# Two-block transformer kernel on one core: norm sums, transposes and up-projections queued at other places among the projections, and the pairs of one attention swapped

## The chip, the cores and the metric

The kernel runs on one core of a Trainium2 chip. The metric is the device time of one launch in microseconds; three runs and one profiled execution of the kernel before are shown.

## What is computed

One sequence of 512 positions of width 1024, all in 32-bit floats, passes two layers of a first block and then one layer of a second block. The change touches the first block alone. Cut to what matters:

```python
def first_block(x, ...):
    for l in range(2):
        h = rms_norm(x, norm1[l])
        a_cq, a_ckv, a_kr, b_q, b_k, b_v, c_q, c_k, c_v, c_qi, c_ki, c_w, d_q, d_k, d_v, d_f = split_cols(h @ w_in[l])
        # A: latent attention, 4 heads
        qa = rms_norm(a_cq, mla_q_norm[l]) @ mla_w_uq[l]
        kv = rms_norm(a_ckv, mla_kv_norm[l]) @ mla_w_ukv[l]
        o_a = causal_block_attention(cat(qa, rope), cat(kv, rope(a_kr)), kv)
        # B: sliding window of 128, sinks
        o_b = sliding_window_attention(rope(b_q), rope(b_k), b_v, swa_sinks[l])
        # C: an indexer picks the 128 best keys of each query
        o_c = dsa_attention(rope(c_q), rope(c_k), c_v, rope(c_qi), rope(c_ki), c_w, top_k=128)
        # D: causal, with the summed log of a forget gate as bias
        o_d = causal_block_attention(d_q, d_k, d_v, log_f_cum=cumsum(log_sigmoid(d_f + fox_b_f[l])))
        x = x + cat(o_a, o_b, o_c, o_d) @ w_out[l]
        h2 = rms_norm(x, norm2[l])
        x = x + square(relu(h2 @ w_up[l])) @ w_down[l]
    return rms_norm(x, final_norm)
```

Every attention has four heads of 64, worked on as two pairs, 0 and 1. The second block (a gated delta rule, dilated window attention, an output projection) follows and is left as it is.

## The kernel before

Activations lie transposed: 128 features on the partitions, 512 positions in the free dimension, so x is eight tiles `xT`. A 32-bit product is made of three matmuls: a weight is split on the chip into a rounded high part `whi` (ScalarE, L130) and the rest `wlo` (VectorE, L133, or GpSimd, L135, by a table `los`), an activation likewise into `hh` and `hl` (`fold`, L166 and L167). `gemm` (L149 to L153) issues high by high, high by low, low by high for each of the `nk` slices of 128: 24 matmuls of 512 columns for an input projection, 6 or 3 for an up-projection of A. Its target comes from `gtile`, three PSUM buffers for all products. Raw weights pass two buffers, split weights three; `rot`, six buffers, holds evacuated projections.

The norm's gain is folded into the activations; the factor per position is applied when a product is evacuated. For it the squares are summed over the tiles on GpSimd (`sumsq_add`, L178), a matmul with ones sums over the partitions (`rstd_rep`, `ssp`, L185; for one column per position `rstd_nat`, `ssn`, L198), and ScalarE makes the root.

The order of the work is that in which the steps are called, refined by a scheduler that goes by priorities: `cur_priority` of the issue, which `later` lowers for a matmul by `self.gp`, so that matmuls with inputs at hand come between those of a step that waits. Each engine works strictly through its resulting list. The steps `e_...` of `attn` are called by the string of names in its last lines. What the change touches among them:

- `e_rstd` makes the norm factor of the layer's start, used by all evacuations.
- `e_small` evacuates `misc` (index keys, gates, rotary key), sums the gates over the positions (L494) and transposes `misc` (`mt`, L501).
- `e_A2` makes A's latents (`latent`, `lat` and their squares `lt`, L606, L609), their norm factors (`rsq`, `rsk`, `rkn`), and the up-projections (`qn`, `kn`, `qr` and four value blocks, L654 to L656), evacuated at L432.
- `e_D(p)` loads, projects and evacuates D's query and key of pair `p`.
- `values` makes the values of D and C (`DV`, `CV`): four blocks of 128 positions, 24 matmuls of 256 columns each (L568 to L572), evacuated by ScalarE (L574).
- `e_Astack`, `e_Cstack`, `e_Dstack` copy a pair's query and key by DMA into a tile `st` and cast them to high and low parts that lie above one another (`qs`, `kh`, `kl`, L364 to L369), so that two matmuls (L392, L393) make a score block. A's low part `al` is made by GpSimd (L676), its scores are at L686.
- `e_topk` picks C's keys with 16 rounds of VectorE instructions for each block of positions (L549 to L551); the result is C's bias, `score[i]`.
- `e_Aatt(p)` to `e_Datt(p)` do the attention of a pair: for each of four blocks and each of two heads scores, bias and row maximum on VectorE (L315), exponential on ScalarE (L316), transposes (L319), product with the values (L328).
- `e_out` makes the output projection from the tiles `mh`, `ml` of the heads and adds it to x (L810). The first half, B and C left out, runs before C's attention, the second half behind it. Each finished `xT` is squared, summed and folded for the feed-forward part, whose first projection starts on the slices that are there; the sum over the partitions (`ssp<-ssq`) comes ahead of it in the program, and the scheduler puts it where its row stands below.

## Time and profile before

| | us |
|---|---|
| runs | 2155.71, 2148.6, 2143.53 |
| median of the runs | 2148.6 |
| the profiled execution | 2142.94 |
| its span on the core | 2141.2 |
| TensorE busy | 2011.2 (94%) |
| VectorE busy | 1303.4 (61%) |
| ScalarE busy | 970.4 (45%) |
| GpSimd busy | 347.0 (16%) |

The rows further down come from this execution. Times are us from the span's start. A timeline row gives start, duration, engine, line, operation and, in brackets, how long the engine had stood idle before it and what ended that. Matmuls overlap, so that one takes longer by its row than the distance to the next. Layer 0 ends at about 672 us, layer 1 at about 1325; each begins with the attention part (some 310 us) and goes on with the feed-forward part.

### The profile page before, as it was taken

The page shows a single profiled execution, that of the slowest core. Times are in us where ns is not written, and L with a number is a line of the kernel's source. Part 1 is how long each engine was busy: PE and PEld are TensorE (multiplying, and loading weights), DVE is VectorE, ACT ScalarE, POOL GpSimd, SP SyncE. Part 2 cuts the span into 40 slices and gives each one's busy share as a digit, 9 for nine tenths or more (in the row PEclk, how much of TensorE's full clock was granted, in tenths as well). Part 3 has the DMA queues.
Part 4 walks back from the last instruction along what each step waited for, and adds up shares of the span by engine and source line. Part 5 has one row for each costly group of instructions (what it writes and reads, how often), then busy time and mean ns, then how long its engine had stood idle before and what let it go on. Part 6 is the DMA issues. An engine that isn't in the chain of part 4 may idle for free.

```text
span 2141.2 us, 27281 instructions
## 1 busy us (share of the span) xinstructions
PE 2011.2 (94%) x10015; PEld 1588.6 (74%) x10015; DVE 1303.4 (61%) x2372; ACT 970.4 (45%) x1769; POOL 347.0 (16%) x282
## 2 busy tenths in 40 slices
PE   7999989999999899999999999899999999999798
PEld 5776768888887676777777888577677677677586
DVE  6598555445435689655665564794694674853664
ACT  4547454233314456554322223654665664735331
POOL 5236320000004227311000001211011011100000
PEclk9999999999999999999999999999999999999899
DMA  6431443233214332343544343232223222344862
GB/s 189 107 103 57 139 142 118 79 99 118 99 59 123 101 101 75 114 159 99 164 131 138 118 138 112 72 96 79 77 70 93 83 73 65 112 128 143 277 219 89
DMA packets 230647, 243.97 MB, mean 114 GB/s; under 512 B 43771, under 2 KB 186026, under 8 KB 230514
## 3 DMA queue, kind: packets, MB, share of 16 engines
q1 hardware_dynamic: 227826, 240.13, 36.4%
q10 hardware_dynamic: 2688, 2.10, 0.3%
q8 instruction: 79, 1.29, 0.3%
q14 instruction: 54, 0.44, 0.1%
HBM read 203.93 MB, written 31.04 MB: 110 GB/s over the span
## 4 chain that ended last, share of the span: by engine, by line
PE 41%; DVE 11%; DMA 5%; ACT 4%; issue 2%; POOL 1%; SPq 0%; DVEq 0%; ACTq 0%; POOLq 0%
PE g L149 10%; PE g L153 10%; PE g L151 10%; DVE wlo L133 2%; ACT whi L130 1%; DMA raw<-in_w_out_dram 1%; PE oT L328 1%; DVE X L1279 1%; DMA raw<-in_ada_w_dram 1%; DVE ada L967 1%; PE oT L1513 1%; DVE pr L1277 1%; PE nt L1174 1%; PE pt L319 1%; PE g L1709 1%
## 5 line engine op out<-in xcount | busy, mean ns | idle before, releaser
L130 ACT ACTIVATE whi<-raw 128x1024 fp32r<-128x1024 f32 (+3 forms) x302 | 297.2, 1000 | 686.4 <-PE g L151 504.0
L149 PE MATMUL g<-hh,whi 128*128 128x512 f32 (+1 forms) x1368 | 548.3, 401 | 5.9 <-ACT whi L130 3.0
L153 PE MATMUL g<-hh,wlo 128*128 128x512 f32 x1368 | 546.3, 399 | 3.9 <-DVE wlo L133 3.9
L151 PE MATMUL g<-hl,whi 128*128 128x512 f32 x1368 | 548.1, 401 | 0.0
L133 DVE TENSOR_TENSOR wlo<-raw,whi 128x1024 fp32r<-128x1024 f32 (+4 forms) x258 | 300.3, 1178 | 108.9 <-ACT whi L130 100.1
L149 PEld LDWEIGHTS g<-hh,whi 128*128 128x128 f32 (+1 forms) x1368 | 260.1, 190 | 63.0 <-issue 4.9
L153 PEld LDWEIGHTS g<-hh,wlo 128*128 128x128 f32 x1368 | 259.8, 190 | 63.0 <-issue 6.5
L151 PEld LDWEIGHTS g<-hl,whi 128*128 128x128 f32 x1368 | 260.4, 190 | 58.0 <-issue 5.6
L149 PE MATMUL g<-sh,whi 128*128 128x512 f32 x512 | 200.6, 392 | 0.0
L151 PE MATMUL g<-sl,whi 128*128 128x512 f32 x512 | 200.2, 392 | 0.0
L153 PE MATMUL g<-sh,wlo 128*128 128x512 f32 x512 | 199.8, 392 | 0.0
L135 POOL TENSOR_TENSOR wlo<-raw,whi 128x1024 fp32r<-128x1024 f32 x44 | 108.0, 2454 | 417.6 <-ACT whi L130 358.9
L890 DVE TENSOR_TENSOR xT<-xT,g 128x512 f32<-128x512 f32 x128 | 87.7, 686 | 136.7 <-PE g L153 136.3
L178 POOL TENSOR_TENSOR ssq<-sq,ssq 128x512 f32<-128x512 f32 x35 | 51.3, 1466 | 436.8 <-ACT sq L177 436.1
L868 DVE SCALAR_TENSOR_TENSOR r<-g,rstd 128x512 f32<-128x512 f32 x64 | 44.2, 691 | 118.5 <-PE g L153 118.0
L153 PEld LDWEIGHTS g<-sh,wlo 128*128 128x128 f32 x512 | 96.4, 188 | 21.1 <-DVE wlo L133 0.7
L149 PEld LDWEIGHTS g<-sh,whi 128*128 128x128 f32 x512 | 96.5, 189 | 20.9 <-issue 0.9
L151 PEld LDWEIGHTS g<-sl,whi 128*128 128x128 f32 x512 | 96.6, 189 | 20.6 <-issue 0.4
L316 ACT ACTIVATE L<-L,mn 128x256 f32<-128x256 f32 (+3 forms) x128 | 68.4, 536 | 19.3 <-DVE mn L315 18.5
L328 PE MATMUL oT<-ptsb,V 128*64 128x128 f32 x592 | 66.9, 287 | 0.1
L324 ACT ACTIVATE ptsb<-pt 128x256 f32<-128x256 f32 (+3 forms) x128 | 51.0, 412 | 32.5 <-PE pt L319 31.6
L149 PE MATMUL g<-yh,whi 128*128 128x512 f32 x112 | 44.7, 404 | 15.7 <-DVE sg L1674 15.7
(447 smaller groups left out, 3318.2 us busy)
## 6 DMA issues: line engine op xcount, KB each, us to landing
raw<-in_w_in_dram SPq DMA_DIRECT2D x46, 1024.0 KB
raw<-in_w_up_dram SPq DMA_DIRECT2D x32, 1024.0 KB
raw<-in_w_down_dram SPq DMA_DIRECT2D x32, 1024.0 KB
raw<-in_ada_w_dram SPq DMA_DIRECT2D x12, 1024.0 KB
raw<-in_w_in_dram SPq DMA_DIRECT2D x22, 512.0 KB
raw<-in_w_out_dram SPq DMA_DIRECT2D x32, 256.0 KB
fd<-f SPq DMA_DIRECT2D x30, 256.0 KB
xd<-xT SPq DMA_DIRECT2D x24, 256.0 KB
```

The source lines that it names most:

```text
L130: nc.scalar.activation(f(hi), src, AF.Copy)
L133: nc.vector.tensor_tensor(f(lw), src, f(hi), ALU.subtract)
L135: nc.gpsimd.tensor_tensor(f(lw), src, f(hi), ALU.subtract)
L149: nc.tensor.matmul(ps, wh, ah, start=first and k == 0, stop=False)
L151: nc.tensor.matmul(ps, wh, al, start=False, stop=False)
L153: nc.tensor.matmul(ps, wl, ah, start=False, stop=last and k == nk - 1)
L178: nc.gpsimd.tensor_tensor(ssq, sq, ssq, ALU.add)
L316: nc.scalar.activation(L[:, :n], L[:, :n], AF.Exp, bias=m, scale=-1.0, accum_out=sm[:, hh, i:i + 1])
L324: nc.scalar.activation(pts_[:, :n], pt[:, :n], AF.Copy)
L328: nc.tensor.matmul(oT[hh * 64:(hh + 1) * 64, i * P:(i + 1) * P], V(hh, j0 + jj), pts[hh][:, jj * P:(jj + 1) * P], start=jj == 0, stop=jj = ...
L868: nc.vector.scalar_tensor_tensor(r, ps, 0.0, rstd, ALU.max, ALU.mult)
L890: nc.vector.tensor_tensor(x, x, ps, ALU.add)
```

## The change

- `gemm` keeps the list of its matmuls, `proj` a list of those lists; `behind(n, m)` issues what stands in it right behind matmul `m` of the `n`-th projection of the layer (both from 0).
- `e_rstd`'s sums come behind matmul 1 of projection 1, the transposes of `misc` behind matmul 20 of projection 4.
- D's load and projections become steps of their own, `Dp:0` and `Dp:1`. `Dp:0` comes before `A2`, whose norm sums are issued behind matmul 4 and one of whose up-projections behind matmul 16 of projection 6, the first of D. The evacuation stays in `D:0`, behind A2 and its stack.
- `values` raises its priority number by one for each block, so that the blocks don't mix.
- C's pair 1 comes before pair 0; the flag `fast` goes with the pair that is now last, and the second half of the output projection takes the tiles in the order 0, 1, 3, 2.
- In the feed-forward part the first chunk issues two projections before its first evacuation, and the norm sum behind matmul 9 of the second.
- `rot` has eight buffers.

```diff
--- before
+++ after
@@ -144,2 +144,3 @@
         old = self.tc.cur_priority
+        mm = []
         for k in range(nk):
@@ -148,8 +149,9 @@
             self.later(old)
-            nc.tensor.matmul(ps, wh, ah, start=first and k == 0, stop=False)
+            mm.append(nc.tensor.matmul(ps, wh, ah, start=first and k == 0, stop=False))
             self.later(old)
-            nc.tensor.matmul(ps, wh, al, start=False, stop=False)
+            mm.append(nc.tensor.matmul(ps, wh, al, start=False, stop=False))
             self.later(old)
-            nc.tensor.matmul(ps, wl, ah, start=False, stop=last and k == nk - 1)
+            mm.append(nc.tensor.matmul(ps, wl, ah, start=False, stop=last and k == nk - 1))
         self.tc.cur_priority = old
+        self.mm = [m.ins for m in mm]
 
@@ -272,3 +274,3 @@
     def rot(self, name):
-        return self.ap.tile([P, T], F32, name=self.nm(name), tag="rot", bufs=6)
+        return self.ap.tile([P, T], F32, name=self.nm(name), tag="rot", bufs=8)
 
@@ -419,4 +421,12 @@
             self.gemm(ps, wv(hi, lw), acts, KD)
+            mms.append(self.mm)
             return ps
 
+
+
+        mms = []
+
+        def behind(n, m):
+            return self.tc.issue_after(mms[n][m])
+
         def pairsel(raw, r, which, nh):
@@ -463,4 +473,5 @@
         def e_rstd():
-            S["rstd"] = rstd = self.rstd_rep([ssq], D, "rstd")
-            S["rnat"] = self.rstd_nat([ssq], D, "rnat", ap)
+            with behind(1, 1):
+                S["rstd"] = rstd = self.rstd_rep([ssq], D, "rstd")
+                S["rnat"] = self.rstd_nat([ssq], D, "rnat", ap)
             for i, (a, b) in enumerate(((self.cos16, "cosr"), (self.sin16, "sinr"))):
@@ -499,4 +510,5 @@
             pt = self.ps.tile([P, T], F32, name=self.nm("mt"), tag="t", bufs=2)
-            for b in range(NB):
-                nc.tensor.transpose(pt[:, HB(b)], misc[:, HB(b)], self.ident)
+            with behind(4, 20):
+                for b in range(NB):
+                    nc.tensor.transpose(pt[:, HB(b)], misc[:, HB(b)], self.ident)
             ptv = pt.rearrange("p (b c) -> p b c", b=NB)
@@ -563,2 +575,3 @@
                 ps = self.gtile()
+                old += 1
                 for k in range(KD):
@@ -617,5 +630,6 @@
             ckvh, sqk = latent(S["ckv"], [gkv[:, l:l + 1]], P)
-            rsq = self.rstd_rep(sqq, MLA_Q, "rsq", pool=ap, tag="tmp", bufs=self.tb)
-            rsk = self.rstd_rep(sqk, P, "rsk", pool=ap, tag="tmp", bufs=self.tb)
-            rkn = self.rstd_nat(sqk, P, "rkn", ap)
+            with behind(6, 4):
+                rsq = self.rstd_rep(sqq, MLA_Q, "rsq", pool=ap, tag="tmp", bufs=self.tb)
+                rsk = self.rstd_rep(sqk, P, "rsk", pool=ap, tag="tmp", bufs=self.tb)
+                rkn = self.rstd_nat(sqk, P, "rkn", ap)
 
@@ -634,3 +648,4 @@
             ps = self.gtile()
-            self.gemm(ps, lambda k: (uh[:, k, 256:384], ul[:, k, 256:384]), lambda k: cqh[k], 2)
+            with behind(6, 16):
+                self.gemm(ps, lambda k: (uh[:, k, 256:384], ul[:, k, 256:384]), lambda k: cqh[k], 2)
             qr_ = evac(ps, "qr_", rsq)
@@ -694,6 +709,8 @@
 
-        def e_D(p):
+        def e_Dp(p):
             raw = self.raw([w_in[:, o + p * P:o + (p + 1) * P] for o in (O_DQ, O_DK)], KD, 256)
-            ts = [evac(proj([(full, raw[:, :, j * P:(j + 1) * P])]), "dq") for j in range(2)]
-            S["D", p] = ts
+            S["D", p] = [proj([(full, raw[:, :, j * P:(j + 1) * P])]) for j in range(2)]
+
+        def e_D(p):
+            S["D", p] = [evac(t, "dq") for t in S["D", p]]
 
@@ -789,6 +806,6 @@
                    lambda h, i, n: self.causal[:, T - n:] if i == 0 else score[i], 64 ** -0.5,
-                   lambda hh, j: VC[:, j, (2 * p + hh) * 64:(2 * p + hh + 1) * 64], fast=p == 1)
+                   lambda hh, j: VC[:, j, (2 * p + hh) * 64:(2 * p + hh + 1) * 64], fast=p == 0)
 
 
-        def e_out(ts, xload, xstore, cols):
+        def e_out(ts, xload, xstore, cols, turn=(0, 1, 2, 3)):
 
@@ -807,3 +824,3 @@
                 ps = self.gtile()
-                self.gemm(ps, lambda k: (hi[:, k, c], lw[:, k, c]), lambda k: S["mix", ts[k]], 4)
+                self.gemm(ps, lambda k: (hi[:, turn[k], c], lw[:, turn[k], c]), lambda k: S["mix", ts[turn[k]]], 4)
                 x = xload(d)
@@ -822,3 +839,3 @@
         env = dict(locals())
-        for s in 'qi misc rstd Aq Ak qi_rope small score:0 A2 Astack:0 D:0 score:1 Aatt:0 score:3 score:2 DV D:1 topk:2 topk:1 topk:3 Astack:1 Dstack:0 Bq Bk Bv Aatt:1 Dstack:1 Datt:0 Bstack:0 Datt:1 Batt:0 Cq Ck Bstack:1 CV Cstack:1 out1:1 out1:3 Batt:1 out1:2 out1:0 Cstack:0 Catt:0 Catt:1'.split():
+        for s in 'qi misc rstd Aq Ak qi_rope small score:0 Dp:0 A2 Astack:0 D:0 score:1 Aatt:0 score:3 score:2 DV Dp:1 D:1 topk:2 topk:1 topk:3 Astack:1 Dstack:0 Bq Bk Bv Aatt:1 Dstack:1 Datt:0 Bstack:0 Datt:1 Batt:0 Cq Ck Bstack:1 CV Cstack:1 out1:1 out1:3 Batt:1 out1:2 out1:0 Cstack:0 Catt:1 Catt:0'.split():
             n, a = (s.split(":") + [None])[:2]
@@ -848,3 +865,3 @@
                 return self.xT[d]
-            self.e_out((2, 3, 4, 5), ld, lambda d, x: self.sumsq_add(ssq2, x, d), range(4))
+            self.e_out((2, 3, 4, 5), ld, lambda d, x: self.sumsq_add(ssq2, x, d), range(4), (0, 1, 3, 2))
             h2 = []
@@ -852,3 +869,3 @@
                 h2.append(self.fold(self.xT[d], self.vec["norm2"][:, l * KD + d:l * KD + d + 1], d))
-            rstd = self.rstd_rep([ssq2], D, "rstd")
+            rstd = None
             NCH = DFF // 512
@@ -858,4 +875,7 @@
             def up(ch):
-                sq = []
-                for f in range(4):
+                nonlocal rstd
+                pss = []
+
+                def project(f):
+                    nonlocal raw
                     if f % 2 == 0:
@@ -864,4 +884,13 @@
                     hi, lw = self.split([(lambda t: t, raw[:, :, (f % 2) * P:(f % 2 + 1) * P])], [P, KD, P])
-                    ps = self.gtile()
-                    self.gemm(ps, lambda k: (hi[:, k, :], lw[:, k, :]), lambda k: h2[k], KD)
+                    pss.append(self.gtile())
+                    self.gemm(pss[f], lambda k: (hi[:, k, :], lw[:, k, :]), lambda k: h2[k], KD)
+                raw, sq = None, []
+                for f in range(4):
+                    if f == len(pss):
+                        project(f)
+                    if rstd is None:
+                        project(1)
+                        with self.tc.issue_after(self.mm[9]):
+                            rstd = self.rstd_rep([ssq2], D, "rstd")
+                    ps = pss[f]
                     r = fp.tile([P, T], F32, name=self.nm("r"), tag="r", bufs=3)
```

`issue_after` puts what is issued in it into the issue order right behind the given instruction.

How the rows of TensorE's list stand at three places of layer 0. First A2 among D's projections. `g` is a product in PSUM with the number of its tile, `hh` and `hl` are high and low part of the folded input, `lat` of the latent, `whi` and `wlo` of a weight; 128x512 is the output. Before:

```order
L149 MATMUL g_451<-hh_182,whi_447 128x512
L151 MATMUL g_451<-hl_183,whi_447 128x512
L149 MATMUL g_636<-lat_581,whi_620 128x512
L532 MATMUL is_546<-ki_533,qi_543 128x256
L532 MATMUL is_552<-ki_533,qi_543 128x384
L149 MATMUL g_653<-lat_581,whi_620 128x512
L151 MATMUL g_636<-lat_581,whi_620 128x512
L153 MATMUL g_636<-lat_581,wlo_621 128x512
...
L151 MATMUL g_636<-lat_587,whi_620 128x512
L153 MATMUL g_636<-lat_587,wlo_621 128x512
L185 MATMUL ssp_597<-lt_579,ones 128x512
```

Now:

```order
L150 MATMUL g_586<-hh_208,whi_582 128x512
L152 MATMUL g_586<-hl_209,whi_582 128x512
L154 MATMUL g_586<-hh_208,wlo_583 128x512
L150 MATMUL g_615<-hh_119,whi_611 128x512
L150 MATMUL g_697<-lat_642,whi_681 128x512
L152 MATMUL g_697<-lat_642,whi_681 128x512
L154 MATMUL g_697<-lat_642,wlo_682 128x512
L150 MATMUL g_697<-lat_648,whi_681 128x512
L152 MATMUL g_697<-lat_648,whi_681 128x512
L154 MATMUL g_697<-lat_648,wlo_682 128x512
L152 MATMUL g_615<-hl_120,whi_611 128x512
L154 MATMUL g_615<-hh_119,wlo_612 128x512
```

Before, the up-projections (`lat`, two of them in turn) begin inside A's last input projection (`g_451`), ahead of any of D; now they stand among D's two projections (`g_586`, `g_615`), one up-projection at a time, and the square sums ahead of them inside `g_586`.

Second, the start of C's attention: `S` is a score block, `kh`, `kl`, `qs` the stacked key and query; kh_2420 belongs to pair 1, kh_2727 to pair 0. Before, among the output projections (`mh`, `ml`):

```order
L151 MATMUL g_2493<-ml_1657,whi_2472 128x512
L153 MATMUL g_2493<-mh_1656,wlo_2473 128x512
L392 MATMUL S_2738<-kh_2727,qs_2726 128x128
L392 MATMUL S_2748<-kh_2727,qs_2726 128x128
L149 MATMUL g_2493<-mh_1830,whi_2472 128x512
L151 MATMUL g_2493<-ml_1831,whi_2472 128x512
L393 MATMUL S_2738<-kl_2728,qs_2726 128x128
L393 MATMUL S_2748<-kl_2728,qs_2726 128x128
```

Now, in the last value block of C (`whi` by `hh`):

```order
L581 MATMUL g_2384<-whi_2297,hh_119 128x256
L583 MATMUL g_2384<-wlo_2298,hh_119 128x256
L394 MATMUL S_2738<-kh_2420,qs_2419 128x128
L394 MATMUL S_2748<-kh_2420,qs_2419 128x128
L585 MATMUL g_2384<-whi_2297,hl_120 128x256
L581 MATMUL g_2384<-whi_2297,hh_130 128x256
L583 MATMUL g_2384<-wlo_2298,hh_130 128x256
L585 MATMUL g_2384<-whi_2297,hl_131 128x256
L395 MATMUL S_2738<-kl_2421,qs_2419 128x128
L395 MATMUL S_2748<-kl_2421,qs_2419 128x128
```

and later pair 0:

```order
L150 MATMUL g_2452<-mh_1830,whi_2431 128x512
L394 MATMUL S_2870<-kh_2727,qs_2726 128x128
L394 MATMUL S_2880<-kh_2727,qs_2726 128x128
L152 MATMUL g_2452<-ml_1831,whi_2431 128x512
L154 MATMUL g_2452<-mh_1830,wlo_2432 128x512
L395 MATMUL S_2870<-kl_2728,qs_2726 128x128
L395 MATMUL S_2880<-kl_2728,qs_2726 128x128
```

The first scores now read pair 1's key and stand 18 matmuls before the end of the value block; pair 0's stand in the second output projection where before they stood in the fourth.

Third, the second norm sum in the first feed-forward projections. Before:

```order
L153 MATMUL g_3226<-hh_3190,wlo_3223 128x512
L149 MATMUL g_3226<-hh_3194,whi_3222 128x512
L185 MATMUL ssp_3214<-ssq_3011,ones 128x512
L151 MATMUL g_3226<-hl_3195,whi_3222 128x512
L153 MATMUL g_3226<-hh_3194,wlo_3223 128x512
L149 MATMUL g_3226<-hh_3198,whi_3222 128x512
```

Now:

```order
L150 MATMUL g_3220<-hh_3210,whi_3216 128x512
L152 MATMUL g_3220<-hl_3211,whi_3216 128x512
L154 MATMUL g_3220<-hh_3210,wlo_3217 128x512
L150 MATMUL g_3249<-hh_3182,whi_3245 128x512
...
L150 MATMUL g_3249<-hh_3194,whi_3245 128x512
L187 MATMUL ssp_3274<-ssq_3011,ones 128x512
L152 MATMUL g_3249<-hl_3195,whi_3245 128x512
L154 MATMUL g_3249<-hh_3194,wlo_3246 128x512
```

The sum stood behind the tenth matmul of the first projection and stands behind the tenth of the second.

## Rows read from the trace of the kernel before

**Rows 1.** Stretches: us, busy us of PE, PEld, DVE, ACT, POOL, clock, DMA, GB/s
```profile
0.00:325.00 325.00, 289.59 (x1570) 224.94 (x1571) 221.60 (x468) 177.19 (x379) 128.28 (x108) 0.95 0.41 121
325.00:672.00 347.00, 347.00 (x1527) 286.63 (x1526) 168.12 (x196) 111.11 (x144) 14.10 (x10) 1.00 0.32 101
672.00:980.00 308.00, 282.83 (x1533) 219.78 (x1532) 208.95 (x454) 164.99 (x362) 110.67 (x85) 0.95 0.36 106
```

**Rows 2.** Waits of PE, whole span: total us, times, longest
```profile
PE ssp L185 <- POOL ssq L178: 11.6, 4, 4.7
PE S L392 <- ACT kh L367: 5.5, 2, 2.8
PE g L149 <- DVE qn L432: 5.5, 2, 2.8
...
PE g L149 <- ACT lat L606: 3.1, 2, 1.5
...
PE S L686 <- POOL al L676: 3.0, 2, 1.5
...
PE S L686 <- DVE mn L315: 2.2, 2, 1.2
PE mt L501 <- issue: 2.1, 1, 2.1
PE mt L501 <- DVE misc L494: 2.0, 1, 2.0
...
PE ssp L185 <- ACT lt L609: 1.9, 2, 0.9
PE S L393 <- POOL kl L369: 1.7, 2, 0.9
```

**Rows 3.** Short stretches behind waits, columns as in rows 1
```profile
134.00:138.00 4.00, 3.94 (x13) 3.65 (x14) 3.79 (x15) 1.48 (x6) 0.00 (x0) 0.50 0.02 4
...
321.00:324.00 3.00, 2.93 (x5) 1.70 (x6) 0.57 (x1) 0.79 (x2) 0.02 (x1) 0.50 0.00 0
...
677.00:681.00 4.00, 4.00 (x14) 3.26 (x15) 0.00 (x0) 1.37 (x4) 2.50 (x2) 0.57 0.00 0
...
728.00:732.00 4.00, 4.00 (x17) 3.61 (x17) 0.93 (x2) 2.08 (x5) 0.00 (x0) 0.50 1.03 231
```

**Rows 4.** Timeline of PE at the start of layer 1: start, us, instruction, idle before
```profile
675.65 0.70 PE L185 MATMUL ssp<-ssq,ones 128*128 128x512 f32 x1 [1.87 <-POOL ssq L178]
```

**Rows 5.** Timeline of DVE and POOL at A2, layer 0
```profile
67.67 2.35 POOL L135 TENSOR_TENSOR wlo<-raw,whi 128x1024 fp32r<-128x1024 f32 x1 [12.29 <-DVE rb L292]
67.69 2.87 DVE L293 TENSOR_TENSOR rb<-qr__135_643,sin 64x512 f32<-64x512 f32 x1
...
72.03 0.69 DVE L432 TENSOR_TENSOR qn<-g,rsq 128x512 f32<-128x512 f32 x1
```

**Rows 6.** Timeline at the second norm sum, layer 0
```profile
319.39 0.70 ACT L166 ACTIVATE hh<-xT,veccol 128x512 fp32r<-128x512 f32 x1
...
320.13 1.44 DVE L167 SCALAR_TENSOR_TENSOR hl<-xT,veccol,hh 128x512 fp32r<-128x512 f32 x1 [0.23 <-ACT hh L166]
...
321.07 2.07 PE L185 MATMUL ssp<-ssq,ones 128*128 128x512 f32 x2 [4.67 <-POOL ssq L178]
...
327.56 0.39 PE L149 MATMUL g<-hh,whi 128*128 128x512 f32 x1
```

**Rows 7.** Timeline at the start of attention C, layer 0
```profile
241.29 1.03 POOL L369 CAST kl<-kl 64x1024 fp32r<-64x1024 f32 x1
...
242.21 0.50 PE L149 MATMUL g<-mh,whi 128*128 128x512 f32 x1 [0.19 <-ACT V L574]
...
254.87 0.69 PE L392 MATMUL S<-kh,qs 128*128 128x128 f32 x2 [2.77 <-ACT kh L367]
```

**Rows 8.** Stretches with top-k rounds, layer 0, columns as in rows 1
```profile
120.00:160.00 40.00, 37.01 (x158) 29.33 (x157) 38.06 (x92) 13.05 (x23) 12.55 (x7) 0.91 0.35 103
...
200.00:236.00 36.00, 35.15 (x229) 26.62 (x230) 31.43 (x92) 18.91 (x55) 11.81 (x7) 1.00 0.19 56
```

More of the change, by code (lines that the diff above doesn't have):

```diff
@@ L692, in e_Aatt @@
                    lambda hh, j: VA[:, j, (2 * p + hh) * 64:(2 * p + hh + 1) * 64])
+        def e_Dp(p):
+            raw = self.raw([w_in[:, o + p * P:o + (p + 1) * P] for o in (O_DQ, O_DK)], KD, 256)
+            S["D", p] = [proj([(full, raw[:, :, j * P:(j + 1) * P])]) for j in range(2)]
         def e_D(p):
-            raw = self.raw([w_in[:, o + p * P:o + (p + 1) * P] for o in (O_DQ, O_DK)], KD, 256)
-            ts = [evac(proj([(full, raw[:, :, j * P:(j + 1) * P])]), "dq") for j in range(2)]
-            S["D", p] = ts
+            S["D", p] = [evac(t, "dq") for t in S["D", p]]
         def e_Dstack(p):
```

## The prediction

> **What bounds the kernel now.** I read four views of the profile, in this order. The table of stretches [rows 1] shows TensorE (PE) at work nearly all the time: in the first feed-forward part, 325 to 672 us, it is busy throughout, 1527 matmuls in 347.00 us, so 0.227 us for each 512-column matmul at full clock and about 0.12 for one of 256. The attention parts of the two layers are the ones with room: 325.00 - 289.59 = 35.4 us without a matmul in the first, 308.00 - 282.83 = 25.2 in the second, and a mean granted clock of 0.95 in both. So PE sets the end, and what the change can win is PE's idle time in the first block and the clock lost behind it. The second block is not touched.
>
> The view of waits names the idle time [rows 2]. Each line has its counterpart in both layers: PE waits for the last square sum (11.6 in four waits), for the casts of a stacked key (5.5 and 1.7), for an evacuated up-projection (5.5), for the normed latent and its squares (3.1 and 1.9), for `misc` (2.0 and 2.1), for the low part of A's stack (3.0). Together 36.4 us. [...] Finally the timelines around four places [rows 4 to 7].
>
> **The change part by part.** The sum is made against the profiled execution, 2142.94 us; the median of the three runs is 2148.6, 5.7 above it.
>
> *Norm sums of a layer's start.* They move 17 matmuls back, about 3.9 us of PE work. In layer 1 PE waited 1.87 us for the sum [rows 4]; 3.9 covers that. The matmuls behind ran at 0.57 for 4.00 us [rows 3], 1.7 lost. Later users of the norm wait for a projection anyway. Layer 0 had only 0.3 (11.6 - 4.7 - 4.7 - 1.9). All of it would be 0.3 + 1.87 + 1.7 = 3.9, without the clock 2.2; I take **3.4**, as PE then has no stop there at all, less a little for what the sums themselves take.
>
> *Transposes of `misc`.* They move behind 12 more matmuls, 2.7 us, against waits of 2.0 and 2.1 [rows 2]: **4.1**, with little doubt, as only the small per-row weights hang on them; if those came late, scores would wait, so the lower end is 2.
>
> *A2 and D.* Before, A's up-projections stand inside its last input projection, ahead of D's two, and PE waits 2.8 + 1.5 + 0.9 = 5.2 us a layer [rows 2]; in layer 1 the clock is then 0.50 for 4.00 us of work [rows 3], 2.0 lost; layer 0 I put at 1.5. After, 48 projection matmuls stand ahead and between, so the inputs are ready. But both `D` tiles now stay in PSUM until A2 has been evacuated, so all up-projections pass one buffer of three: matmuls, evacuation, next. An evacuation takes 0.69 [rows 5]; with the tail of the last matmul I count 1.1. Four projection matmuls between cover 0.9, eleven 2.5, none nothing: three waits of 0.2, one of 1.1, and about 1 for the value blocks behind ScalarE, 2.7 in all. I keep 0.7 of the clock loss. So 5.2 + 1.5 - 3.4 = 3.3 and 5.2 + 2.0 - 3.4 = 3.8, **7.1**. Upper end: no new wait, 13.9. Lower end: a DVE instruction beside POOL's 2.35 us cast took 2.87 instead of 0.69 [rows 5]; two of them more on that chain in each layer take 8.8 off and leave -1.7.
>
> The raw weights of `D` are asked for earlier on SP's queue, those of A2 and the last three copies of the index stack later; the index scores are then some 1.2 us later, but stand deeper among projections, which cover them. At nothing.
>
> *V blocks whole, and A's second pair.* The four V blocks of `DV` now run one after another; fewer fillers stand among the first pair's scores. The second pair's scores start 29 rows, some 6.6 us of PE work, later, which covers the 1.5 us wait for POOL's low part [rows 2]; behind it 2.0 us are lost to the clock [rows 3]. Upper end 2 x 3.5 = 7; lower end 0, as a wait for row maxima (2.2 in two [rows 2]) can grow while DVE is busy 38.06 of 40 us [rows 8]. I take 2 a layer, **4**.
>
> *C's pairs swapped.* Before, PE waits 2.77 us for the high part of pair 0's key and 0.85 (half of 1.7) for the low one [rows 2, 7]. After, pair 1 comes first, and its scores are put into the last V block. Its key's second half is ready at 241.29 + 1.03 = 242.3; PE, which starts the output projection at 242.21 [rows 7], would be 18 matmuls of 0.12 ahead of that, at 239.9: a new wait of 2.4. Pair 0 comes later by one pair's first scores, but sooner than its own key: I count 0.9 and 1.7. That is 5.0 against 3.6, offset by copies that no longer stand behind two stores on SP's queue. **0**, between -6 and +11 for both layers: all of the new against the old, or all gone and 2.0 of clock each.
>
> *Second norm sum.* Before, PE stops behind the tenth matmul of the first feed-forward projection for 4.67 us, until the sum arrives, and runs its next 2.93 us at 0.50 [rows 3, 6]. Now it goes on, until it needs the last folded row: its high part ends at 319.39 + 0.70 = 320.1, its low part at 320.13 + 1.44 = 321.6 [rows 6]. So two waits of some 1.3 us stay, the second projection starts at about 322.3 instead of 327.56, and the sum itself still takes 1.0 there (2.07 at half clock). Gain 5.3 - 1.0 = 4.3; with half clock in 3 us of it 2.8. I take 3.5, twice: **7**.
>
> *Eight rotary buffers* and the changed turn of the sums remove waits only; nothing.
>
> *What is lost on the way.* Up to C, DVE is busy 31.43 of 36 us [rows 8], and the casts of C's keys hang on it. PE arrives there some 8 us earlier in layer 0, and what DVE can't follow comes back as a wait. I take 2 a layer, **-4**.
>
> Sum: 3.4 + 4.1 + 7.1 + 4 + 0 + 7 - 4 = 21.6, so 2142.9 - 21.6 = **2121 us**.
>
> [...]
>
> **The rivals.**
> 1. *All named waits go.* The 36.4 us of [rows 2] and nine half-clock stretches in the attention parts, four of them in [rows 3], at some 1.5 each: 2142.9 - 50 = 2093. For it: the moves are made at just these places. Against: the last folded row and the keys of C are late by themselves [rows 6, 7].
> 2. *The leads are given back at C.* PE waits until DVE and POOL have C's keys; then only the second sum, `misc` in part and layer 1's start remain: 7 + 2 + 3 = 12, 2131. For it: DVE at 0.87 before C. Against: DVE's own waits before C are for PE, so it can move up too.
> 3. *A2 stays at half clock* through the short stops: 2.4 more lost in each layer, 2126. [...]
> 4. *Slower.* The first pair of A has eight score blocks whose maxima DVE makes between top-k rounds, and DV's blocks no longer stand between them. If each block then waits 1.5 us, with a half-clock stretch of 2.0 for every second one, a layer loses 20; two lose 40 and beat the 25.6 won elsewhere: 2143 + 14 = 2157. It decides from about 1 us a block on. Against: the second `D` pair's projections and the index scores fill the place.
> 5. *The change doesn't do what it says:* the order on PE moved as described, so only in that the waits move along: 2143.
>
> **How the numbers follow.** Forecast, 2110 to 2130 (the terms of A2 and C half way to their ends, the others together 1.5 either way): 0.45; rival 1: 0.10; rival 2: 0.20; rival 3: 0.10; rival 4: 0.05; rival 5: 0.10. A measurement of this kernel can tell about 0.5% from no change, so faster means below 2137.9 by the median. The forecast and rivals 1, 2 and 3 lie there, but for a third of rival 2's spread: 0.45 + 0.10 + 0.13 + 0.10 = 0.78. Same: 0.07 + 0.10 = 0.17; slower 0.05. The range leaves out rival 4, half of rival 1 and some of rival 5, whose single time is its upper edge: 2095 to 2143.
>
> **What would show it.** In the changed kernel PE's waits for `misc` and for the first norm sum should be gone; the waits for up-projections be several below 1.2 us; at the second norm sum PE should wait about 1.3 for a high and 1.3 for a low folded part, and the granted clock there be above 0.7; at C a wait for POOL's key of pair 1 should appear. The prediction is wrong if layer 0's attention, up to the first feed-forward part, does not end 8 to 15 us sooner, if waits for row maxima grow by more than 5 us, or if the A2 stretches show a granted clock near 0.5 for more than 3 us.

## The result and the profile after

The changed kernel takes 2121.91 us, the median of four runs from 2117.55 to 2123.68, against 2148.3 before; the ratio is 0.9872, with a 95% interval of 0.9852 to 0.9892. That is 1.3% faster. In a later set of rounds it took 2121.83 us, at 0.9887 (0.9858 to 0.9916). The profiled execution has a span of 2121.4 us, 19.8 below that of before.

PE's waits in the changed kernel (whole span; us in total, times, longest):

```profile
PE g L150 <- DVE sg L1703: 16.5, 1, 16.5
PE S L395 <- POOL kl L371: 6.7, 5, 1.6
PE S L701 <- DVE mn L317: 5.4, 2, 2.7
...
PE S L395 <- POOL qk L385: 3.1, 2, 1.9
...
PE g L669 <- DVE kn L442: 1.8, 2, 0.9
...
PE S L701 <- POOL al L691: 1.5, 2, 0.7
...
PE S L394 <- ACT kh L369: 1.3, 2, 0.7
...
PE g L150 <- DVE qn L442: 0.4, 2, 0.2
```

The waits for the square sum (11.6 before), for `misc` (4.1) and for the latent and its squares (5.0) are gone; those for an up-projection fell from 5.5 to 0.4 and, at the value blocks, 1.8, those for the high part of a key from 5.5 to 1.3 [rows 2]. POOL's low key part is now waited for 6.7 us, where it was 1.7: 6.1 of it at C, 0.6 at one place of B. The wait for row maxima at A has grown from 2.2 to 5.4. The first row lies in the second block and stands in both kernels (15.7 before).

The stretches (us; busy us of PE, PEld, DVE, ACT, POOL; granted clock; DMA; GB/s), first whole attention parts, then short ones:

```profile
0.00:316.00 316.00, 290.18 (x1579) 224.88 (x1580) 221.33 (x468) 176.63 (x378) 127.99 (x108) 0.97 0.42 125
...
660.00:956.00 296.00, 280.09 (x1549) 216.91 (x1548) 206.28 (x456) 165.30 (x362) 111.93 (x86) 0.98 0.37 113
```

```profile
60.00:80.00 20.00, 19.08 (x78) 13.25 (x76) 11.17 (x21) 9.22 (x19) 1.56 (x1) 1.00 0.54 143
80.00:90.00 10.00, 9.34 (x72) 8.85 (x73) 5.39 (x5) 4.87 (x9) 5.98 (x3) 1.00 0.21 53
...
136.00:140.00 4.00, 4.00 (x13) 3.42 (x12) 2.76 (x10) 0.99 (x4) 0.00 (x0) 0.50 0.20 69
312.00:316.00 4.00, 1.95 (x5) 1.35 (x6) 2.26 (x2) 1.64 (x3) 1.40 (x1) 0.81 0.01 4
316.00:320.00 4.00, 4.00 (x13) 2.91 (x12) 1.22 (x1) 0.44 (x1) 0.00 (x0) 0.77 0.26 48
664.00:668.00 4.00, 4.00 (x19) 3.02 (x19) 0.45 (x1) 1.41 (x3) 1.85 (x2) 1.00 0.12 45
```

Without a matmul are 316.00 - 290.18 = 25.8 us of layer 0's attention part, where it was 35.4, and 296.00 - 280.09 = 15.9 of layer 1's, where it was 25.2 [rows 1]. The clock is 0.97 and 0.98 after 0.95. In A2 (60 to 90 us) and at the start of layer 1 (664 to 668) it is 1.00 now; behind A's row maxima (136 to 140) it is 0.50 still, as in [rows 3].

Where the time came from shows best at marks that both traces have. Each mark is the start of one instruction in PE's timeline, the folded rows' in DVE's; "lead" is by how much it comes sooner. A modulation sum is a small matmul for the second block, placed in layer 1's feed-forward part.

| mark | before | changed | lead | won since the mark above |
|---|---|---|---|---|
| layer 0: first matmul of D's values | 87.44 | 82.19 | 5.2 | 5.2 |
| first matmul of C's values | 230.34 | 224.12 | 6.2 | 1.0 |
| last folded row | 320.13 | 313.06 | 7.1 | 0.9 |
| last feed-forward product | 670.66 | 660.65 | 10.0 | 2.9 |
| layer 1: first matmul of D's values | 742.52 | 722.13 | 20.4 | 10.4 |
| first matmul of C's values | 885.16 | 865.24 | 19.9 | -0.5 |
| last folded row | 974.80 | 953.84 | 21.0 | 1.0 |
| first modulation sum | 1007.27 | 983.12 | 24.1 | 3.2 |
| last modulation sum | 1271.05 | 1247.13 | 23.9 | -0.2 |
| last output product | 2133.21 | 2113.46 | 19.8 | -4.2 |

So the starts of the two layers give 15.6 of the 24 us won in the first block, the second norm sums 6, and all of the attention between them 2.4. Four us are lost in the part that was not changed; by the medians of the runs, 2148.3 - 2121.9 = 26.4 us were won, so they are this pair of executions' own.

The second norm sum in the changed kernel, layer 0, by the timeline (start, us, engine, instruction, idle before):

```profile
312.31 0.71 ACT L168 ACTIVATE hh<-xT,veccol 128x512 fp32r<-128x512 f32 x1
...
313.06 1.44 DVE L169 SCALAR_TENSOR_TENSOR hl<-xT,veccol,hh 128x512 fp32r<-128x512 f32 x1 [0.24 <-ACT hh L168]
...
313.07 0.49 PE L150 MATMUL g<-hh,whi 128*128 128x512 f32 x1 [1.20 <-ACT hh L168]
...
314.55 0.80 PE L152 MATMUL g<-hl,whi 128*128 128x512 f32 x1 [0.98 <-DVE hl L169]
...
315.57 0.63 PE L150 MATMUL g<-hh,whi 128*128 128x512 f32 x1
...
318.95 1.02 PE L187 MATMUL ssp<-ssq,ones 128*128 128x512 f32 x2
```

PE does not stop for the sum, which now stands at 318.95, but for the last folded row, 1.20 us for its high and 0.98 for its low part. The second projection begins at 315.57, 2.5 us behind the start of the low part, where it was 7.4 [rows 6].

A2 and the start of C in PE's timeline, and POOL's at C:

```profile
74.07 0.47 PE L150 MATMUL g<-lat,whi 128*128 128x512 f32 x1 [0.19 <-DVE qn L442]
...
80.15 0.36 PE L669 MATMUL g<-whi,lat 128*128 128x256 f32 x1 [0.88 <-DVE kn L442]
```

```profile
233.85 0.41 PE L394 MATMUL S<-kh,qs 128*128 128x128 f32 x2 [0.69 <-ACT kh L369]
...
236.27 0.69 PE L395 MATMUL S<-kl,qs 128*128 128x128 f32 x2 [1.49 <-POOL kl L371]
```

```profile
235.18 1.03 POOL L371 CAST kl<-kl 64x1024 fp32r<-64x1024 f32 x1
```

The up-projections that pass one PSUM buffer cost stops of 0.19 and 0.88 us. At C the low part of pair 1's key ends at 235.18 + 1.03 = 236.2, and PE's second set of score matmuls starts behind it, after 1.49 us of standing idle. With 0.69 for the high part and 1.56 for pair 0's low part, PE waits 3.7 us for C's keys in layer 0; before it was 2.77 + 0.85 = 3.6.

### The profile page after: what moved, and what is told of

It is laid out like the page before. It is cut to its first block, busy times and chain, and to the rows that moved or that the text cites. A ratio compares the mean times of both kernels' runs of the same rounds, so it can differ in the third digit from the quotient of the medians.

```text
span 2121.4 us, 27312 instructions
## 1 busy us (share of the span) xinstructions
PE 2008.2 (95%) x10015; PEld 1584.1 (75%) x10015; DVE 1299.5 (61%) x2372; ACT 970.4 (46%) x1769; POOL 346.6 (16%) x282
## 4 chain that ended last, share of the span: by engine, by line
PE 68%; DVE 14%; DMA 7%; ACT 5%; issue 3%; POOL 1%; SPq 1%; DVEq 0%; ACTq 0%; POOLq 0%
PE g L150 17%; PE g L152 17%; PE g L154 17%; DVE wlo L133 3%; PE oT L330 2%; PE pt L321 1%; ACT whi L130 1%; DVE X L1308 1%; DMA raw<-in_w_out_dram 1%; DMA raw<-in_ada_w_dram 1%; DVE ada L996 1%; PE oT L1542 1%; DMA st<-c 1%; DVE m L561 1%; DVE sc L562 1%
## 5 line engine op out<-in xcount | busy, mean ns | idle before, releaser
L133 DVE TENSOR_TENSOR wlo<-raw,whi 128x1024 fp32r<-128x1024 f32 (+3 forms) x258 | 306.3, 1203 | 114.6 <-ACT whi L130 106.1
L154 PEld LDWEIGHTS g<-hh,wlo 128*128 128x128 f32 x1368 | 259.7, 190 | 62.5 <-issue 6.9
```

What stands on the lines that cost most here:

```text
L133: nc.vector.tensor_tensor(f(lw), src, f(hi), ALU.subtract)
L154: mm.append(nc.tensor.matmul(ps, wl, ah, start=False, stop=last and k == nk - 1))
```

## The experiments

Parts of the change were undone one at a time, one part was put into the kernel before alone, and three versions try what the new waits point at. Times of different rounds are compared by their ratio to the kernel before in the same rounds. A single ratio is sure to some 0.2%, 4 us; the marks of the profiles tell smaller effects apart, where stages in the same order repeat: from the last feed-forward product of layer 0 to the first matmul of D's values in layer 1 the changed kernel needs 61.48 us, and eight other profiles with the same order there 61.46 to 61.99. Other stages repeat less well. From D's values to C's values all kernels but the last one below take 140.3 to 144.9 us, and from C's values to the last folded row all that make C's low key part on POOL take 88.0 to 92.6; smaller differences are not told apart there by one profile.

**A2 back ahead of D.**

```diff
-... score:0 Dp:0 A2 Astack:0 D:0 ...
+... score:0 A2 Astack:0 Dp:0 D:0 ...
-            with behind(6, 4):
-            with behind(6, 16):
```

> The changed kernel with A2 put back ahead of D's projections (its norm sums and up-projections no longer placed among them); all else stays. Theory (the terms add): the waits for the up-projections (2.8 us a layer), for the latent (1.5) and its squares (0.9) come back with a half-clock stretch behind them, so the first value block of D starts about 3.5 us later in layer 0 and the time is 6 to 9 us above the changed kernel's 2122. Rival (slack: what is won early is waited for again at C's keys, where the changed kernel waits 3.0 us a layer for POOL): the C waits shrink by as much, and the time rises by 0 to 3 us only.

2138.17 us, ratio 0.9945 (0.9932 to 0.9959): 0.0073 above the changed kernel's first ratio, some 16 us. The stage named above takes 66.98 us, 5.5 more, and in layer 0 the part from the transposes of `misc` to D's values 39.03 instead of 32.80. PE's waits in layer 1's attention part:

```profile
PE S L395 <- POOL qk L385: 4.4, 1, 4.4
...
PE g L150 <- DVE qn L442: 2.8, 1, 2.8
PE g L150 <- ACT lat L619: 1.5, 1, 1.5
PE S L699 <- POOL al L689: 1.5, 1, 1.5
PE S L699 <- DVE mn L317: 1.4, 1, 1.4
...
PE ssp L187 <- ACT lt L622: 0.9, 1, 0.9
```

The three waits of before are back, 2.8, 1.5 and 0.9. The rival falls: nothing is given back at C, where PE waits 4.2 us for keys in layer 0, not less than the 3.7 of the changed kernel. The theory is short by half: beside A2's own stages (6.2 and 5.5) the copy in D's stack on POOL is waited for 4.0 and 4.4 us in the two layers, where the changed kernel waits 3.1 in both together. The kernel before waited only 1.3 and 0.6 there, so undoing this part alone overstates what it is worth. And the waits at A's second pair are 1.5 for the low part and 1.4 for row maxima, nearly as before (1.5 and 1.2 in this layer), not 0.7 and 2.7: what happens at that pair comes from the A2 part.

**A2's part alone, put into the kernel before** (with eight rotary buffers).

```diff
-... score:0 A2 Astack:0 D:0 ... DV D:1 ...
+... score:0 Dp:0 A2 Astack:0 D:0 ... DV Dp:1 D:1 ...
+            with behind(6, 4):
+            with behind(6, 16):
-        return self.ap.tile([P, T], F32, name=self.nm(name), tag="rot", bufs=6)
+        return self.ap.tile([P, T], F32, name=self.nm(name), tag="rot", bufs=8)
```

> The kernel before with the A2 part alone (D's projections ahead, norm sums and one up-projection placed among them, eight rotary buffers). Theory (its worth is large by itself): the waits of 5.2 us a layer go, layer 1's start up to D's first value block falls from 71.9 to 65 to 67 us, and the time is 9 to 14 us below the kernel before. Rival (the parts need each other: without the later transposes PE stops there, and without the later scores what is won is waited for at C): 4 to 7 us below.

2138.87 us against 2149.13, ratio 0.9958 (0.9942 to 0.9974): 10 us of gain (9 by the ratio, whose interval is 6 to 12 and so doesn't shut out the rival's 4 to 7), and 66.62 us in layer 1's stage, as the theory has it. PE's waits in layer 1's attention part and at the norm sum behind it:

```profile
PE ssp L187 <- POOL ssq L180: 6.8, 2, 4.9
...
PE S L696 <- DVE mn L317: 2.7, 1, 2.7
PE mt L509 <- issue: 2.1, 1, 2.1
...
PE S L696 <- POOL al L686: 0.7, 1, 0.7
```

Here the value blocks are interleaved as before and C's pairs stand as before; the waits at A's second pair are those of the changed kernel, 2.7 and 0.7. That the value blocks cover them, as the prediction said, is not so. In layer 0, from the transposes to D's values, it is 36.67 us where the kernel before needs 39.51: 2.8 won, although this execution lost 1.7 us to a half clock behind the wait for `misc` (0.57 from 52 to 56 us), where the kernel before ran at 1.00. So this part is worth 2.8 and 5.2 us when added alone, 6.2 and 5.5 when undone. Which of its moves does it, D's projections ahead or the sums and the up-projection among them, was not tried.

**The transposes of `misc` back.**

```diff
-            with behind(4, 20):
+            if True:
```

> The changed kernel with the transposes of misc back at their old place. Theory (terms add): the wait of 2.0 and 2.1 us comes back, +4 us, no half-clock stretch. Rival (slack later): projections behind it shield A2 from its own waits, so a stop here makes the latents come in time and the time rises by under 2 us.

2119.43 us, ratio 0.9863 (0.9840 to 0.9885): by the time no difference can be told. By the stage of layer 1, 62.90 us, it is worth 1.4 there.

```profile
PE mt L513 <- issue: 2.1, 1, 2.1
```

The wait of 2.1 is back; one of 0.7 for the index scores' query, which the changed kernel has in this place, goes. So the theory's size is a third too large in that layer. In layer 0, from the first product with `wlo` (at 18.50 us in the changed kernel) to D's values, it is 65.23 us, after 63.69 in the changed kernel and 62.5 to 63.5 in the nine other profiles that have the transposes and A2 where it has them: at least 1.5 more. Together that is some 3 us, nearer to the theory's 4 than to the rival's less than 2.

**The first norm sums back.**

```diff
-            with behind(1, 1):
+            if True:
```

> The changed kernel with the norm sums of a layer's start back at their old place. Theory: in layer 1 a wait of 1.9 us and a half-clock stretch of some 1.5 us return, in layer 0 0.3 us: +3 to +4 us. Rival: PE has more projections ready and the norm is needed by DVE only later, so under +1.5 us.

2126.36 us, ratio 0.9878 (0.9856 to 0.9901). The time again tells little; the stage of layer 1 takes 67.07 us, 5.6 more, which is against the rival. The wait and the stretches behind it (columns as above):

```profile
PE ssp L187 <- POOL ssq L180: 1.9, 1, 1.9
```

```profile
668.00:672.00 4.00, 4.00 (x14) 3.19 (x13) 0.00 (x0) 1.56 (x4) 0.58 (x1) 0.50 0.01 4
672.00:676.00 4.00, 4.00 (x13) 3.15 (x13) 0.65 (x1) 0.93 (x1) 1.94 (x2) 0.69 0.00 0
```

1.9 us of wait and 4.00 x 0.50 + 4.00 x 0.31 = 3.2 of clock make 5.1 of the 5.6. In the kernel before the same wait was followed by 1.7 of lost clock [rows 3], and so it was in the kernel with A2's part alone (0.57 from 677 to 681 us): the wait repeats, the length of the half-clock stretch does not.

**The second norm sum back ahead of the projections.**

```diff
-            rstd = None
+            rstd = self.rstd_rep([ssq2], D, "rstd")
...
-                    if rstd is None:
-                        project(1)
-                        with self.tc.issue_after(self.mm[9]):
-                            rstd = self.rstd_rep([ssq2], D, "rstd")
```

> The changed kernel with the second norm sum issued ahead of the feed-forward projections again. Theory: the wait of 4.7 us for the last square sum and its half-clock stretch come back in both layers, +6 to +7 us together (net 2.9 and 3.2 a layer by the traces). Rival (the folded rows bind anyway): the waits of 1.2 and 1.0 us for the last folded row are what counts, and the time rises by less than 3 us.

2129.49 us, ratio 0.9901 (0.9885 to 0.9918), 0.0029 above the first ratio of the changed kernel, some 6 us, though the two intervals overlap. PE waits for the sum as it did, in layer 0

```profile
PE ssp L187 <- POOL ssq L180: 5.3, 1, 5.3
```

and in layer 1 4.6. From the last folded row to the last feed-forward product it is 349.94 us against 347.59, 2.4 more in layer 0, and 32.18 against 29.28 up to the first modulation sum, 2.9 more in layer 1. The marks separate the two orders: the three profiles with the sum ahead take 349.9 to 350.6 and 32.2 to 32.7 us, the eleven with it behind 346.1 to 348.9 and 27.7 to 29.3. The theory holds by them; the rival does not.

**The value blocks interleaved again.**

```diff
-                old += 1
```

> The changed kernel with the four value blocks interleaved again (priority not raised per block). Theory: it moves the second pair of A earlier, so that the wait for POOL's low part of A (0.7 now, 1.5 before) comes back and the time rises by 1 to 4 us. Rival (whole blocks cost fillers): the wait for row maxima at A's scores, 2.7 us a layer in the changed kernel against 1.0 before, goes away and the time falls by 2 to 5 us.

2126.62 us, ratio 0.9876 (0.9857 to 0.9896): the same. PE's waits at A in layer 1:

```profile
PE S L700 <- DVE mn L317: 2.7, 1, 2.7
...
PE S L700 <- POOL al L690: 0.7, 1, 0.7
```

Both are those of the changed kernel, and layer 0 has the same 2.7, so neither theory nor rival has it right: this line moves neither wait, and the time by nothing that can be measured.

**C's pairs back.**

```diff
-... Cstack:0 Catt:1 Catt:0
+... Cstack:0 Catt:0 Catt:1
-... fast=p == 0)
+... fast=p == 1)
-... range(4), (0, 1, 3, 2))
+... range(4))
```

> The changed kernel with C's pair 0 first again, with the flag and the order of the sums as before. Theory (the swap only trades waits): PE waits for pair 0's key again, 3.6 us or a little more a layer, in place of 3.0 for pair 1's; the time is within 0 to +4 us of the changed kernel. Rival (the swap is what lets the lead through): PE reaches pair 0's scores 6 us earlier than before while its key does not come earlier, so the wait grows to 8 us or more a layer and the time rises by 10 us or more.

2120.49 us, ratio 0.9864 (0.9849 to 0.9879): the same. PE's waits at C, layer 0:

```profile
PE S L394 <- ACT kh L369: 3.4, 1, 3.4
...
PE S L395 <- POOL kl L371: 1.8, 2, 1.2
```

0.6 of the 1.8 lies at B. At C it is 3.4 and 1.2 us in place of 0.7 for the high and 3.0 for the low part of a key. The swap trades one wait for the other, as the theory has it.

**Six rotary buffers.**

```diff
-        return self.ap.tile([P, T], F32, name=self.nm(name), tag="rot", bufs=8)
+        return self.ap.tile([P, T], F32, name=self.nm(name), tag="rot", bufs=6)
```

> The changed kernel with six rotary buffers. Theory (as forecast: they cost nothing and win little): within 2 us of the changed kernel. Rival (they are what lets D's tiles be evacuated while A2's are still in use): evacuations of D wait for a buffer, PE waits at the products behind them, and the time rises by 4 us or more.

2114.81 us, ratio 0.9841 (0.9817 to 0.9865). Not slower, and the stage of layer 1 takes 61.62 us, so the rival falls. By the ratio it is 7 us faster, which is more than the theory's 2; whether six are better is not settled, as the interval overlaps that of the changed kernel.

**The changed kernel again.**

> The changed kernel once more, on the chip and in the rounds of the three beside it, with a second profile. Theory (what differs between executions is the clock behind waits, not the order): its stages from the first matmul of the second block on differ from the first profile by some us (866 us there from the last modulation sum to the last output product), while layer 1's start up to D's first value block is again 61.5 us, within 0.3; the time is 2117 to 2127. Rival: the stages repeat within 0.3 us everywhere, so that stage differences of 3 us between the kernels are real.

2121.83 us. Layer 1's start takes 61.53 us, after 61.48. From the last modulation sum to the last output product it is 870.5 us (1242.14 to 2112.60), after 866.3; before 862.2, and in the other kernels, all with the same code there, 861.6 to 871.5. So the theory holds: the 4.2 us lost in the second block are no effect of the order. The whole stretch in the kernel before, in the changed kernel and in its repetition (columns as above):

```profile
1271.05:2133.21 862.16, 805.00 (x4137) 625.25 (x4137) 527.42 (x989) 430.09 (x773) 93.93 (x79) 0.98 0.37 113
```

```profile
1247.13:2113.46 866.33, 807.43 (x4138) 626.99 (x4137) 528.09 (x989) 429.79 (x773) 93.85 (x79) 0.97 0.37 112
```

```profile
1242.14:2112.60 870.46, 812.18 (x4138) 630.09 (x4137) 528.16 (x989) 430.09 (x773) 93.97 (x79) 0.97 0.36 112
```

PE stands idle 57.2, 58.9 and 58.3 us, and is busy 805.0, 807.4 and 812.2 for the same matmuls, at a mean clock of 0.98, 0.97 and 0.97. So 2.4 of the 4.2 us are slower matmuls and 1.7 longer waits; between the two executions of the changed kernel the matmuls take 4.8 us more and the waits 0.6 less.

**C's low key part on DVE.**

```diff
+        if kv:
+            for r in (slice(0, 64), slice(64, 128)):
+                nc.vector.tensor_tensor(kl[r, :nk], st[64:128, :nk], kh[64:128, :nk], ALU.subtract)
+            return q, kh, kl
         (eng or nc.gpsimd).tensor_tensor(kl[0:64, :nk], st[64:128, :nk], kh[64:128, :nk], ALU.subtract)
         nc.gpsimd.tensor_copy(kl[64:128, :nk], kl[0:64, :nk])
...
-            S["C", p] = self.stack(st, eng=eng("C"))
+            S["C", p] = self.stack(st, eng=eng("C"), kv=True)
```

> The changed kernel with the low key part of C's stacks made on DVE, both halves by subtraction, in place of a 2.4 us subtraction and a 1.0 us copy on POOL; the values are the same. Theory (at C PE waits for POOL's work alone, 3.0 us a layer): these waits shrink to under 1 us each layer and the time falls by 3 to 6 us. Rival (DVE or the high part is as late): a wait for the high part or for row maxima takes their place, and the time stays within 2 us.

2115.07 us, ratio 0.9824 (0.9803 to 0.9846). At C no wait for `kl` is left (B's stacks stay on POOL, with one wait of 0.6); what leads PE's waits in layer 1 now is

```profile
PE S L705 <- DVE mn L317: 2.7, 1, 2.7
PE S L399 <- POOL qk L389: 2.3, 1, 2.3
```

From C's values to the last folded row it takes 85.55 and 85.40 us in the two layers, after 88.94 and 88.60: 6.6 us together, just above the theory's 3 to 6. Both stages lie below the 88.0 to 92.6 of the kernels with POOL's keys. By the ratio it is 10 us.

**The same with C's pair 0 first** (the edits of "C's pairs back" and of the run above).

> The changed kernel with the low key part of C's stacks made on DVE and C's pair 0 first again. Theory (the swap only trades waits): within 3 us of the version with the swap and DVE keys (2115 in its own rounds). Rival (the swap pays once POOL is out of the way, since pair 0's high part is late by its copies): a wait of 3 us a layer for the high part stays, and the time is 5 to 8 us above that version.

2116.88 us, ratio 0.9853 (0.9826 to 0.9881). By the medians that is 2 us above the version with the swap, as the theory has it, by the ratios 6 us, as the rival has it; the intervals overlap, so the time doesn't decide. A wait for the high part of the key stays in layer 1:

```profile
PE S L398 <- ACT kh L369: 2.4, 1, 2.4
```

With 2.0 in layer 0 it is nearer to the rival's 3 us than to nothing; by the stages, 85.95 and 87.25 us, it costs 0.4 and 1.9. So the swap may be worth some 2 us once POOL is out of the way, which is not sure, and before that it can't be told from nothing.

**C's keys on DVE, with the swap, and D's stack copied on ScalarE.**

```diff
-        nc.gpsimd.tensor_copy(kl[64:128], kl[0:64])
+        nc.scalar.activation(kl[64:128], kl[0:64], AF.Copy)
```

> The changed kernel with the low key part of C's stacks on DVE, and the copy within D's stacks on ScalarE in place of POOL. Theory: the waits for D's low key part on POOL (1.0 and 2.3 us in the version with C's keys on DVE) go, and the time falls by 1 to 4 us more, to 2110 to 2116. Rival (ScalarE's list holds the copy back behind exponentials): a wait for ScalarE takes their place and nothing is won.

2104.05 us, ratio 0.9797 (0.9773 to 0.9820), against 0.9887 (0.9858 to 0.9916) for the changed kernel in the same rounds: 18 us faster than it, and 45 than the kernel before. That is more than the theory's 2110 to 2116. PE's first waits in layer 1:

```profile
PE S L705 <- DVE mn L317: 2.7, 1, 2.7
PE is L548 <- POOL qi L542: 1.8, 3, 1.1
```

No wait for POOL's copy is left. From D's values to C's values it takes 139.13 and 138.58 us, after 141.75 and 144.91 in the version with C's keys on DVE alone: 2.6 and 6.3 us, where the waits themselves were 1.0 and 2.3. In layer 1 that version ran at 0.86 in the 25 us around this place, this one at 1.00, so in this pair of executions a half-clock stretch went with the wait. Both times lie below all others of this stage, 140.3 to 144.9, but by 1.2 and 1.7 us only: how much of the gain repeats was not tried.

ScalarE does not make this copy faster than POOL, 1.06 us against 1.03. In layer 1, with C's keys on DVE alone, POOL

```profile
798.73 0.88 POOL L737 TENSOR_SCALAR db<-crep,cumn 128x128 f32<-128x128 f32 x1 [5.57 <-DMA crep<-cumd]
...
800.54 1.03 POOL L389 CAST qk<-qk 64x1024 fp32r<-64x1024 f32 x1
```

and with D's copy on ScalarE

```profile
792.04 1.06 ACT L389 ACTIVATE qk<-qk 64x1024 fp32r<-64x1024 f32 x1
```

But DVE's part of the key was there at 797.84 and POOL began 2.7 us later, as the copy stood behind D's bias (`db`), which had waited for a transfer; in the other version DVE's part was there at 791.45 and ScalarE began 0.6 us later.

## Why the prediction was right

The forecast was 2121, the time is 2122. The sum was 21.6 against one execution; the spans differ by 19.8, the medians by 26.4, the first block by 24. The main mechanism is right: stops of PE at the starts of the layers and at the second norm sum went, and with them most of the half clock behind them: the granted clock is 1.00 at the start of layer 1 and in that layer's A2, where it was 0.57 and 0.50, and 0.81 and 0.77 at the second norm sum of layer 0, where it was 0.50. That the number is within 1 us is in part luck, as the execution it starts from was a quick one: from the median of before, 2148.6, the same sum gives 2127. Its steps did not all come out so well.

- *Starts of the layers* (3.4 + 4.1 + 7.1 = 14.6): 15.6 by the marks. Within it the sizes were off. A2 is worth 2.8 and 5.2 when added alone, 6.2 and 5.5 when undone, for 3.3 and 3.8: the prediction charged 2.7 us a layer for the one PSUM buffer and kept 0.7 of the clock loss; the stops were 0.19 and 0.88 in layer 0, and the clock 1.00. The first norm sums are worth 5.6 in layer 1 when undone, not 3.1, since the half-clock stretch behind the wait was longer there (3.2 us lost, for 1.7). The transposes are worth 1.4 in layer 1 and some 1.5 in layer 0, not 2.05. Undone singly these make 12.5 in layer 1, while together they win 10.4 there, so they are not independent; the sum came out because the errors had both signs. By the times, A2 undone and the second norm sum undone make 16 + 6 = 22 of the 26 us; no other part undone singly can be told from nothing by its time.
- *V blocks and A's second pair* (4): this step failed. The line on the value blocks does nothing that can be measured. That pair's wait for POOL does shrink, from 1.5 to 0.7, but the wait for row maxima grows from 1.0 and 1.2 to 2.7, and both follow from A2, as A2 alone and A2 undone show. Won up to C: 1.0 and -0.5 in this pair of executions, in which a loss for DVE is already contained; the stage varies by more than that.
- *C's pairs* (0) and *what is lost on the way* (-4): the wait for pair 1's key stands where it was foreseen, 0.69 + 1.49 = 2.2 us in layer 0 for 2.4, and pair 0's key is waited for 1.56, for 2.6. Together 3.7 for 3.6 before, so 0 is right. (The lower end of -6 does not come out of the prediction's own numbers: 5.0 against 3.6 is -2.8 in two layers.) Won from C on 0.9 and 1.0, less than this stage varies, and nothing was taken back: undoing A2 made C no quicker. The -4 has no counterpart of its own; with the 4 above it cancels, which is luck.
- *Second norm sum* (7): 2.9 and 3.2 by the marks, 2.4 and 2.9 when undone; the waits of 1.3 and 1.3 are 1.20 and 0.98, and the clock 0.81 and 0.77 there, as said.
- *Rotary buffers* (0): the eight win nothing that can be seen; six were not slower, and whether they are quicker is open.
- *Second block* (0): -4.2 in this pair of executions, 2.4 of it by the clock and 1.7 by waits; the repeated profile shows that it is no effect of the change.

Of the signs named ahead, one failed narrowly: layer 0's attention ended 7.1 us sooner, not 8 to 15 (8.6 in the repeated profile). The others came out: row maxima are waited for 3.2 us more, not 5. Rival 1 is out, as the last folded row (1.20 and 0.98) and C's keys (3.7 in layer 0) are still waited for. Rival 4 is out, with one wait of 2.7 us for row maxima at A in a layer in place of one at each block, and rival 5, as the waits went. Rival 2 (leads given back at C) is out by the A2 run. Rival 3 is out for this case: with stops of 0.19 and 0.88 us at A2 the granted clock stayed at 1.00 from 60 to 90 us, and with 0.2 and 0.9 in layer 1 it was 1.00 from 705 to 725. Its 2.4 us a layer were the author's estimate, and no run shows them.

## What to carry to other kernels

Here a small matmul that waited for another engine's sum held up what stood behind it in the matmul engine's list, for 4.67 us in one place and 1.87 in another [rows 4, 6]: put such a matmul as far back as its users allow, and fill the gap with products whose inputs are long there. Price a wait with the half-clock stretch that can follow it, which here cost up to 3.2 us behind 1.9 us of waiting, but don't count on its length: behind the same wait 1.7 us were lost in two other profiles. Undo a part and add it alone before you give it a price: A2's part was worth 16 us by the time when taken out and 9 when put in alone. Then look for what is waited for next and whether another engine can have it ready sooner, by a shorter operation or by a shorter queue ahead of it: here three small operations taken off GpSimd won 18 us more, where the whole change had won 26.

## What was not expected of the hardware

- The same instructions with nearly the same waits differ by several us between executions: the second block took 861.6 to 871.5 us from one mark to another in thirteen profiles other than that of before, while the start of layer 1, where no wait of the changed kernel is above 0.9 us, repeated within 0.6 us in nine.
- C's low key part took POOL 2.37 + 1.03 us, a subtraction of one half and a copy; DVE made both halves by subtraction in 2.46 us, and no wait for it is left at C. The copy alone is no quicker on ScalarE, 1.06 us.
